# Two of four weight sums by accumulating DMAs, six feed-forward blocks begun early, GpSimd left with transfers

## The chip, the cores and the metric

One core of a Trainium2 chip runs the whole program. Its engines work side by side and wait for one another at semaphores: TensorE (PE, with its weight loads, PEld), VectorE (DVE), ScalarE (ACT), GpSimd (POOL) and SyncE (SP, which only issues transfers). SP's transfers and POOL's transfers are two queues; each is issued in order. The metric is the device time in microseconds (us), a median over runs.

## The reference, cut to what matters

```python
h = rms_norm(x, g_pre_mix) * (1.0 + scale_m) + shift_m          # x: 512 tokens x 2048
o = concatenate([mla_mixer(...), gla_mixer(...)]) @ w_out       # attention and a chunked recurrence
x = x + gate_m * rms_norm(o, g_post_mix)
h = rms_norm(x, g_pre_ffn) * (1.0 + scale_f) + shift_f          # "the second norm"
f = (silu(h @ w_ffn_gate) * (h @ w_ffn_up)) @ w_ffn_down        # 2048 -> 5632 -> 2048
x = x + gate_f * rms_norm(f, g_post_ffn)
```

The six vectors shift, scale and gate come from `silu(c) @ w_ada + b_ada`, 96 rows of 128 outputs. All is float32.

## The kernel before, in words

Every large product is made of float32r matmuls: each operand is split into a rounded part and a rest, and `mm3` (L212 to L216) issues three matmuls for one. A weight tile is split by `wparts` (L902 to L906): ACT casts 128x1024 floats into the rounded part, DVE subtracts (L905) to get the rest. The parts lie in a ring of eight `wh` tiles of 1024 columns. A weight block is loaded by `raw_of` (L908 to L911), 1 MB on SP's queue, into a ring of four `wr` tiles. All other tiles of 512 columns come out of one pool of 73 (`t2`).

The feed-forward products are done by a seven-product scheme (Strassen-Winograd) on 2x2 blocks. The products of the up stage are called q1, q2, q5, r7, r6, q4, r3. q1 and q2 need the first half of the tokens and the weights as they are (b11, b21). For the others sums of the weights are made in place in the `wr` tiles, in this order of use: q5 needs b11+b12, r7 needs b12+b22, r6 needs b11+b12+b22, q4 needs all of them plus b21, and r3 needs b22 as it is. These are the "four sums of weights". Two are on DVE (`vadd`, L924) and two on POOL (`padd`, L921).

The program, in the order in which it is written (a scheduler then interleaves the engines' lists):

- Up to about 765 us: conditioning rows (`ada`, one load and one DVE reduction each, 64 of them handed out by `next(more)` beside the later projections), projections, attention, recurrence, and the first half of the output product.
- `out_group` (L875): the output product, for two tokens' tiles at a time, with the running squares and a product with the gate row on POOL (L887). `second_norm` (L793) follows for each token tile: it scales on DVE (L811), transposes on PE (L814), and its rows go through ACT (L820). `first_forms` and `more_forms` make seven token forms with their two parts, 56 tiles of the pool.
- The early loop (L928): for the first `PRO` blocks of 22, q1 and q2 alone, which need the first two token tiles only, with steps of the second norm and of the forms (`advance`) written in between. Its weights are loaded once more when the block is finished.
- The up loop (L969): per block two halves s of up to seven products, 2.87 us of PE each; after every two blocks `pair_forms` writes seven forms in two parts (14 tiles `gd`, 256 KB each) to memory through POOL's queue.
- The down loop (L1029): five groups of four blocks, each in two halves p of seven products. `back` (L1023, its transfer L1025) reads the 28 `gd` tiles of a group through SP's queue; the weights' sums are like those above, in 128x2048 tiles, two on DVE and two on POOL.
- The tail (L1074 on): the last two blocks by plain products, with the weights' rests made on POOL (L1084), the gate product on POOL (L1102), and the output.

Of the kernel before, what the change touches and what calls it, by code (L numbers as in the profile page):

```python
# [11 lines left out]
F32 = mybir.dt.float32  # L12
# [17 lines left out]
NBLK = DFF // 256  # L30
PRO = 2
ATT_SCALE = 192.0 ** -0.5
# [45 lines left out]
def block_kernel(ctx, tc, x, c, pos, w_ada, cols, w_g1, w_kqvr, w_uq, w_uk, w_uv, wg17,  # L78
# [373 lines left out]
    def fill_qk():  # L452
        for half in range(2):
            pss = [bank("A") for _ in range(4)]
            for kq in (2, 3):
                w = load_split(w_kqvr[half, kq], 4, 512)
                for k, b in ORDER[kq == 3]:
                    mm3(pss[b], cut(w[k], b * P, P), hT[4 * kq + k], kq + k == 2, kq + k == 6)
                if kq == 3:
                    add_up(pss, qk[4 * half:4 * half + 4])  # L460
                    qk[4 * half:4 * half + 4] = spill(qk[4 * half:4 * half + 4], "qk")
                yield

    def fill_vr():
        for ci in range(4):
            pss = [bank("A") for _ in range(4)]
            k0 = 2 if ci < 2 else 0
            for kq in range(k0, 4):
                w = load_split(w_kqvr[2 + ci, kq], 4, 512)
                for _ in range(4):  # L470
                    next(more)
# [22 lines left out]
    def fill_out():  # L494
# [3 lines left out]
        for i, (n, q) in enumerate(todo):  # L498
            w = ahead
            if i < 7:  # L500
                ahead = load_split(w_out[todo[i + 1]], 4, 512)
            for _ in range(2):
                next(more)
# [289 lines left out]
    def second_norm(t):  # L793
# [15 lines left out]
        for n in range(4):  # L809
            y = t2()  # L810
            V.tensor_scalar(y, og[t][n], v2, None, op0=ALU.mult)  # L811
            ps = bank("B")
# [62 lines left out]
    def out_group(n, toks, steps=0):  # L875
# [7 lines left out]
        for t in toks:  # L883
            o = og[t][n] = fetch(og[t][n])
            V.tensor_tensor(out=o, in0=pss[t], in1=o, op=ALU.add)
            A.activation(pss[t], o, AF.Square, accum_out=osum[:, 4 * t + n:4 * t + n + 1])
            nc.gpsimd.tensor_tensor(out=o, in0=o, in1=ggm[n], op=ALU.mult)  # L887

# [31 lines left out]

    def padd(out, a, b):  # L921
        nc.gpsimd.tensor_tensor(out=out, in0=a, in1=b, op=ALU.add)  # L922

# [4 lines left out]
    for j in range(PRO):  # L928
        raws = [raw_of(w_fg[j, s]) for s in range(2)]
        q1, sg = t2(), t2()  # L930
        for f, o in (("a11", 0), ("a12", 1024)):
            ps = bank("A")
            for s in range(2):
                up_product(ps, wparts(raws[s][:, o:o + 1024]), f, s, s == 0, s == 1)
                advance(2 if j == 0 else 3)
            if f == "a11":
                A.copy(out=q1, in_=ps)
# [31 lines left out]
    for j in range(NBLK):  # L969
        pss = {}  # L970
        for s in range(2):
            gr, ur = raw_of(w_fg[j, s]), raw_of(w_fu[j, s])
            b11, b21, b12, b22 = gr[:, :1024], gr[:, 1024:], ur[:, :1024], ur[:, 1024:]

            def product(name, f, src, tag):
# [14 lines left out]
            else:  # L990
                q1, sg = early[j]
            vadd(b11, b11, b12)
            padd(b12, b12, b22)
            product("q5", "s1", b11, "A")
# [3 lines left out]
            if s == 1:  # L998
# [4 lines left out]
                vadd(c22, pss["q5"], w_)  # L1003
            padd(b11, b11, b21)
            product("q4", "a22", b11, "B")
# [17 lines left out]
    def back(d):  # L1023
        t = t2(F32R)
        dma(out=t.bitcast(F32), in_=d)  # L1025
        return t

    acc = [[{} for _ in range(2)] for _ in range(2)]
    for c_ in range(NBLK // 4):  # L1029
        fs = {}  # L1030
        for p in range(2):
# [19 lines left out]
            product("q2", "a12", b21)  # L1051
            padd(b11, b11, b12)
            padd(b12, b12, b22)
            product("r3", "s4", b22)
# [22 lines left out]
    for n in range(4):  # L1077
        raw = raw_of(w_fl[n])
        row = []
        for k in range(4):  # L1080
            hi, lo = t2(F32R), t2(F32R)
            r = raw[:, k * 512:(k + 1) * 512]
            A.copy(out=hi, in_=r)
            nc.gpsimd.tensor_tensor(out=lo, in0=r, in1=hi, op=ALU.subtract)  # L1084
            row.append((hi, lo))
        wl.append(row)
    fsum = cp.tile([P, 4 * NT + 1], F32, name="fsum")
    for t in range(NT):
# [5 lines left out]
        for j, (n, o, w) in enumerate(parts_):  # L1094
# [6 lines left out]
            A.activation(sq, f, AF.Square, accum_out=fsum[:, 4 * t + j:4 * t + j + 1])  # L1101
            nc.gpsimd.tensor_tensor(out=f, in0=f, in1=ggf[n][:, o:o + w], op=ALU.mult)  # L1102
        v = small(1, "v1")
# [62 lines left out]
```

## Time and profile before

| | us |
|---|---|
| median of 3 runs | 2258.38 (2248.99 to 2261.52) |
| the profiled execution, its own time | 2255.43 |
| its span, first to last instruction | 2253.7 |

| engine | busy us | share |
|---|---|---|
| PE | 2109.3 | 94% |
| PE weight loads | 1851.7 | 82% |
| DVE | 1764.0 | 78% |
| ACT | 907.7 | 40% |
| POOL | 540.4 | 24% |

The span leaves 1.7 us of the profiled time outside. A busy PE is not PE at full rate, since matmuls overlap and the granted clock varies; so a view of stretches also counts the matmuls in each, and a stretch in which they are densest serves as the measure of what PE could have done.

### The profile page before, as it was taken

Reading aid. Unit: us, or ns where it says so; the run is one execution under the profiler, and the core shown is the slowest. Engines: PE = TensorE matmul, PEld = TensorE weight load, DVE = VectorE, ACT = ScalarE, POOL = GpSimd, SP = SyncE. Lnnn points to the kernel's source line nnn. Section 1 sums busy time; section 2 is a strip of 40 time slices with the busy share of each in tenths; the row PEclk is TensorE's granted clock in tenths of the full one; section 3 lists DMA queues with packets and bytes.
Section 4 is the critical chain, followed back from the end, with each engine's and each line's share of the span. In section 5 each row is a group of like instructions: output and inputs, shape, how many; then the busy total and the mean of one; then the engine's idle time right before and its main releaser. Section 6 shows DMA issues by size and latency. Waiting matters only on the chain. (4 is left out here: it accounts for less than half of the span.)

```text
span 2253.7 us, 32197 instructions
## 1 busy us (share of the span) xinstructions
PE 2109.3 (94%) x12714; PEld 1851.7 (82%) x12714; DVE 1764.0 (78%) x2095; ACT 907.7 (40%) x1265; POOL 540.4 (24%) x436
## 2 busy tenths in 40 slices
PE   7999999996999967999999999999999799999977
PEld 5888777773888867999999999999999687777866
DVE  6885787886475778888888888887887669888984
ACT  5433222324233664444434434434444353333332
POOL 0000000000212332323333333333332232131136
PEclk9999999996999979999999999999999999999989
DMA  8882586885575742434434424433433647564334
GB/s 333 317 306 100 210 306 246 316 311 199 187 247 202 260 178 75 178 133 158 160 122 149 173 113 146 178 113 141 178 128 125 244 178 273 213 217 148 128 131 150
DMA packets 91578, 432.18 MB, mean 192 GB/s; under 512 B 12168, under 2 KB 12280, under 8 KB 54817
## 3 DMA queue, kind: packets, MB, share of 16 engines
q1 hardware_dynamic: 69840, 360.09, 44.0%
q0 software_dynamic: 21584, 70.02, 8.1%
q8 instruction: 100, 1.64, 0.3%
q14 instruction: 52, 0.43, 0.1%
q10 hardware_dynamic: 2, 0.01, 0.0%
HBM read 370.80 MB, written 59.26 MB: 191 GB/s over the span
## 5 line engine op out<-in xcount | busy, mean ns | idle before, releaser
L905 DVE TENSOR_TENSOR wh<-wr,wh 128x1024 fp32r<-128x1024 f32 x448 | 677.8, 1524 | 214.7 <-ACT wh L904 210.3
L904 ACT CAST wh<-wr 128x1024 fp32r<-128x1024 f32 x448 | 464.6, 1050 | 649.0 <-PE ps L215 247.1
L214 PE MATMUL ps<-t,wh 128*128 128x256 f32 x2464 | 705.1, 286 | 18.8 <-ACT wh L904 9.0
L216 PE MATMUL ps<-t,wh 128*128 128x256 f32 x2464 | 704.9, 286 | 12.1 <-DVE wh L905 11.9
L215 PE MATMUL ps<-t,wh 128*128 128x256 f32 x2464 | 703.6, 286 | 4.4 <-DVE t L832 4.4
L214 PEld LDWEIGHTS ps<-t,wh 128*128 128x128 f32 x2464 | 479.0, 194 | 22.5 <-ACT wh L904 11.4
L216 PEld LDWEIGHTS ps<-t,wh 128*128 128x128 f32 x2464 | 478.7, 194 | 15.5 <-DVE wh L905 15.2
L215 PEld LDWEIGHTS ps<-t,wh 128*128 128x128 f32 x2464 | 479.0, 194 | 5.8 <-DVE t L832 5.7
L922 POOL TENSOR_TENSOR wr<-wr 128x1024 f32<-128x1024 f32 x88 | 223.5, 2540 | 500.5 <-DVE wh L905 232.1
L228 DVE CUSTOM_DVE_ANT_0 wr<-wr,cB 128x2048 f32<-128x2048 f32 x96 | 219.2, 2285 | 41.1 <-DMA wr<-w_ada 41.0
L215 PE MATMUL ps<-wh,t 128*128 128x512 f32 x560 | 222.9, 398 | 22.1 <-DVE wh L905 22.1
L214 PE MATMUL ps<-wh,t 128*128 128x512 f32 x560 | 221.4, 396 | 11.4 <-DMA t<-gd 11.3
L216 PE MATMUL ps<-wh,t 128*128 128x512 f32 x560 | 219.9, 395 | 0.5 <-DMA t<-gd 0.5
L202 ACT CAST hi<-wr 128x1024 fp32r<-128x1024 f32 (+3 forms) x122 | 122.7, 1010 | 223.1 <-PE ps L215 134.1
L203 DVE TENSOR_TENSOR lo<-wr,hi 128x1024 fp32r<-128x1024 f32 (+3 forms) x122 | 145.1, 1193 | 67.0 <-ACT hi L202 66.5
L215 PE MATMUL ps<-t,hi 128*128 128x512 f32 x432 | 173.0, 400 | 3.1 <-DVE t L302 3.0
L922 POOL TENSOR_TENSOR wr<-wr,wr 128x2048 f32<-128x2048 f32 x20 | 102.6, 5129 | 303.1 <-DVE wh L905 198.7
L216 PE MATMUL ps<-t,lo 128*128 128x512 f32 x432 | 170.4, 395 | 0.0
L214 PE MATMUL ps<-t,hi 128*128 128x512 f32 x432 | 168.7, 398 | 1.3 <-ACT t L300 1.3
L214 PE MATMUL ps<-hi,t 128*128 128x512 f32 x400 | 161.4, 404 | 1.0 <-DVE t L209 0.9
L925 DVE TENSOR_TENSOR wr<-wr,wr 128x1024 f32<-128x1024 f32 (+1 forms) x108 | 153.3, 1420 | 5.5 <-DMA wr<-w_fu 3.2
L215 PE MATMUL ps<-lo,t 128*128 128x512 f32 x400 | 156.6, 392 | 0.3 <-DVE lo L203 0.3
(230 smaller groups left out, 2656.6 us busy)
## 6 DMA issues: line engine op xcount, KB each, us to landing
wr<-w_ada SPq DMA_DIRECT2D x96, 1024.0 KB, 5.8
wr<-w_fg SPq DMA_DIRECT2D x48, 1024.0 KB, 5.0
wr<-w_fu SPq DMA_DIRECT2D x44, 1024.0 KB, 7.2
wr<-w_fd SPq DMA_DIRECT2D x40, 1024.0 KB, 4.9
gd<-t POOLq DMA_DIRECT2D x148, 256.0 KB, 2.6
t<-gd SPq DMA_DIRECT2D x148, 256.0 KB, 5.3
wr<-w_kqvr SPq DMA_DIRECT2D x24, 1024.0 KB, 4.9
wr<-w_out SPq DMA_DIRECT2D x22, 1024.0 KB, 5.5
```

The source lines that it names most:

```text
L202: A.copy(out=hi[:, :n], in_=r)
L203: V.tensor_tensor(out=lo[:, :n], in0=r, in1=hi[:, :n], op=ALU.subtract)
L214: T.matmul(ps, lhsT=a, rhs=c_, start=start, stop=False)
L215: T.matmul(ps, lhsT=a, rhs=d_, start=False, stop=False)
L216: T.matmul(ps, lhsT=b, rhs=c_, start=False, stop=stop)
L228: V.tensor_tensor_reduce(out=raw, in0=raw, in1=cB, scale=1.0, scalar=0.0, op0=ALU.mult, op1=ALU.add, accum_out=adac[:, j:j + 1])
L904: A.copy(out=hi, in_=src)
L905: V.tensor_tensor(out=lo, in0=src, in1=hi, op=ALU.subtract)
L922: nc.gpsimd.tensor_tensor(out=out, in0=a, in1=b, op=ALU.add)
L925: V.tensor_tensor(out=out, in0=a, in1=b, op=ALU.add)
```

## The change

Accumulating DMAs (`plus`: a transfer on POOL's queue that adds what it reads from memory into the tile) make two of the four sums: b12+b22 and b11+b12, the addend being read from the weights in memory once more. They are issued on POOL's queue. The other two are DVE's. POOL has no arithmetic left: the gate products and the rests of the tail go to DVE, and the scaling by the second norm's factor goes from DVE to ACT. `back` is issued on POOL's queue instead of SP's. `PRO` is 6 instead of 2, with two steps of the norm at each place of the early loop. 16 of the 64 `ada` steps are handed out earlier, beside four sweeps that had none.

```diff
-PRO = 2
+PRO = 6
@@ fill_qk
                 w = load_split(w_kqvr[half, kq], 4, 512)
+                for _ in range(4):
+                    next(more)
@@ fill_vr
-                for _ in range(4):
+                for _ in range(3):
                     next(more)
@@ fill_out
-            for _ in range(2):
+            for _ in range(1 + q):
                 next(more)
@@ second_norm
-            V.tensor_scalar(y, og[t][n], v2, None, op0=ALU.mult)
+            A.activation(y, og[t][n], AF.Copy, scale=v2)
@@ out_group
-            nc.gpsimd.tensor_tensor(out=o, in0=o, in1=ggm[n], op=ALU.mult)
+            V.tensor_tensor(out=o, in0=o, in1=ggm[n], op=ALU.mult)
-    def padd(out, a, b):
-        nc.gpsimd.tensor_tensor(out=out, in0=a, in1=b, op=ALU.add)
+    def plus(out, src):
+        dma2(out=out, in_=src, accum_op=ALU.add)
@@ early loop
-                advance(2 if j == 0 else 3)
+                advance(2)
@@ up loop
             b11, b21, b12, b22 = gr[:, :1024], gr[:, 1024:], ur[:, :1024], ur[:, 1024:]
+            plus(b12, w_fu[j, s, :, 1024:])
@@
-            vadd(b11, b11, b12)
-            padd(b12, b12, b22)
+            plus(b11, w_fu[j, s, :, :1024])
             product("q5", "s1", b11, "A")
             product("r7", "s3", b12, "A")
             vadd(b11, b11, b22)
             product("r6", "s2", b11, "B")
@@
-            padd(b11, b11, b21)
+            vadd(b11, b11, b21)
             product("q4", "a22", b11, "B")
@@ back
-        dma(out=t.bitcast(F32), in_=d)
+        dma2(out=t.bitcast(F32), in_=d)
@@ down loop
-            padd(b11, b11, b12)
-            padd(b12, b12, b22)
+            plus(b11, w_fd[c_, 0, 2 * p + 1])
+            plus(b12, w_fd[c_, 1, 2 * p + 1])
             product("r3", "s4", b22)
@@ tail
-            nc.gpsimd.tensor_tensor(out=lo, in0=r, in1=hi, op=ALU.subtract)
+            minus(lo, r, hi)
-            nc.gpsimd.tensor_tensor(out=f, in0=f, in1=ggf[n][:, o:o + w], op=ALU.mult)
+            V.tensor_tensor(out=f, in0=f, in1=ggf[n][:, o:o + w], op=ALU.mult)
```

## Rows read from the trace of the kernel before

**Rows 1.** Stretches: length, PE (matmuls), PEld, DVE, ACT, POOL busy, clock, DMA, GB/s.

```profile
800.00:950.00 150.00, 119.77 (x875) 114.25 (x874) 124.51 (x158) 73.42 (x126) 44.42 (x35) 0.89 0.42 153
950.00:1000.00 50.00, 50.00 (x418) 50.00 (x417) 37.96 (x34) 21.05 (x24) 12.88 (x5) 1.00 0.28 106
950.00:1730.00 780.00, 765.69 (x6290) 761.75 (x6289) 647.14 (x607) 333.42 (x383) 256.67 (x201) 0.99 0.39 143
1750.00:1800.00 50.00, 37.16 (x174) 29.82 (x172) 35.12 (x28) 20.80 (x28) 14.08 (x10) 0.93 0.62 234
1800.00:2140.00 340.00, 323.61 (x1396) 264.79 (x1397) 285.81 (x237) 130.66 (x134) 80.68 (x16) 0.98 0.54 195
2120.00:2140.00 20.00, 20.00 (x90) 16.57 (x89) 19.76 (x24) 8.06 (x8) 0.00 (x0) 1.00 0.61 211
2140.00:2190.00 50.00, 40.01 (x168) 31.81 (x166) 46.97 (x49) 19.02 (x27) 12.92 (x4) 0.94 0.34 126
2190.00:2254.00 64.00, 49.05 (x203) 36.99 (x203) 27.61 (x57) 13.68 (x39) 42.05 (x37) 0.90 0.41 148
```

**Rows 2.** The hole of the second norm, same columns as rows 1.

```profile
820.00:845.00 25.00, 10.31 (x55) 8.62 (x55) 17.42 (x27) 19.74 (x49) 7.83 (x6) 0.61 0.49 191
```

**Rows 3.** SP's issues around it: start, us, queue, line, tile from source.

```profile
781.16 10.36 SPq L799 DMA_DIRECT2D wr<-x  x2
799.21 14.84 SPq L910 DMA_DIRECT2D wr<-w_fg  x3
```

**Rows 4.** PE's waits from 960 to 1720: us in total, times, longest.

```profile
PE ps L216 <- DVE wh L905: 9.1, 9, 1.0
PE ps L214 <- ACT wh L904: 5.2, 9, 0.6
```

**Rows 5.** PE's waits from 1720 on, same columns.

```profile
PE ps L215 <- DVE wh L905: 22.1, 12, 3.8
PE ps L215 <- POOL t L1084: 11.4, 12, 8.3
PE ps L214 <- DMA t<-gd: 11.3, 2, 6.5
```

**Rows 6.** POOL and DVE in order of time, in an up block (start, us).

```profile
1000.23 2.40 POOL L922 TENSOR_TENSOR wr<-wr 128x1024 f32<-128x1024 f32 x1 [6.79 <-issue]
...
1000.62 3.10 DVE L905 TENSOR_TENSOR wh<-wr,wh 128x1024 fp32r<-128x1024 f32 x1
...
1005.56 1.22 DVE L905 TENSOR_TENSOR wh<-wr,wh 128x1024 fp32r<-128x1024 f32 x1
```

**Rows 7.** POOL and DVE near the end of the down stage (start, us).

```profile
2143.86 12.11 POOL L922 TENSOR_TENSOR wr<-wr,wr 128x2048 f32<-128x2048 f32 x2 [36.94 <-DVE wh L905]
...
2147.11 9.94 DVE L905 TENSOR_TENSOR wh<-wr,wh 128x1024 fp32r<-128x1024 f32 x2
```

**Rows 8.** Groups by line and form: count, busy us, mean ns, idle before.

```profile
L922 POOL TENSOR_TENSOR wr<-wr 128x1024 f32<-128x1024 f32 x88 | 223.5, 2540 | 500.5 <-DVE wh L905 232.1 <-DVE wr L925 175.2 <-issue 93.0
L922 POOL TENSOR_TENSOR wr<-wr,wr 128x2048 f32<-128x2048 f32 x20 | 102.6, 5129 | 303.1 <-DVE wh L905 198.7 <-DMA wr<-w_fd 72.1 <-DMA t<-gd 31.6
L228 DVE CUSTOM_DVE_ANT_0 wr<-wr,cB 128x2048 f32<-128x2048 f32 x96 | 219.2, 2285 | 41.1 <-DMA wr<-w_ada 41.0
```

**Rows 9.** Transfers: SP's queue (packets, MB, share); issues with KB and us to landing.

```profile
q1 hardware_dynamic: 69840, 360.09, 44.0%
...
wr<-w_fu SPq DMA_DIRECT2D x44, 1024.0 KB, 7.2
...
gd<-t POOLq DMA_DIRECT2D x148, 256.0 KB, 2.6
```

**Rows 10.** SP's issues where the down stage begins, two of ten rows.

```profile
1748.36 10.64 SPq L1025 DMA_DIRECT2D t<-gd  x12
1777.95 0.33 SPq L910 DMA_DIRECT2D wr<-w_fd  x1
```

**Rows 11.** POOL in the tail, in order of time.

```profile
2191.80 19.85 POOL L1084 TENSOR_TENSOR t<-wr,t 128x512 fp32r<-128x512 f32 x16
```

## The prediction

> **What bounds the kernel now.** I read the stretches first. PE is busy nearly everywhere, so the question is how far each stretch is from PE's own best. In 950 to 1000 us there are 418 matmuls of 256 columns in 50 us without a gap, 0.1196 us each; in 2120 to 2140, in the down stage, 90 of 512 columns in 20 us, 0.222 us each [rows 1]. These two are the measure: a stretch's length less its count times the measure is what it loses, be it in gaps, in a lower granted clock or in loose pairs. All numbers are of the profiled execution (2255.4 us; span 2253.7, 1.7 outside), 3 us under the median of 2258.4.
>
> - 800 to 950, second norm and first up blocks: 875 matmuls at 0.1196 make 104.7 of 150 us: **45 lost**.
> - 950 to 1730, the up loop: 6290 make 752 of 780: **28 lost**.
> - 1750 to 1800, up to down: 51 of the 174 are still of the small kind: 6.1 + 123 x 0.222 = 33.4 of 50: **17 lost**.
> - 1800 to 2140, down: 1396 x 0.222 = 310 of 340: **30 lost**.
> - 2140 to 2190: 168 x 0.222 = 37.3 of 50: **13 lost**. From 2190 PE's work is some 43 us (203 matmuls, 24 of them small) and ends about 2245, so **12 lost**.
>
> That is 145 us, all in stretches that the change touches. Then the waits: who ends them.
>
> **The early blocks.** From 820 to 845 PE is busy 10.3 of 25 us, at a granted clock of 0.61 on average, so between its levels of 1.2 and 2.4 GHz [rows 2]: the two early blocks are used up and the forms of the last two token tiles aren't made. An early block is 96 small matmuls (2 products x 2 halves x 24), 11.5 us; four more are 46 us of work that waits for none of those forms, against 45 lost. They cost 8 more loads of 1 MB, beside other work. What limits them is buffers: of four wr tiles two hold x from its issue at 781 to 791 until the norm is done, and the weights of the early blocks come in late, three issues from 799 to 814 [rows 3]. So not all of the hole fills: **28 gained**, bounds 8 (only what two wr tiles bring in time) and 42. DVE's y (16 scalings) going to ACT and the gate products coming from POOL (16) cancel on DVE; ACT has room there, 73.4 of 150 us busy [rows 1].
>
> **The sums in the up loop.** A POOL sum of 1024 columns takes 2.54 us, 88 times [rows 8], and DVE's subtraction issued beside one takes 3.10 us instead of 1.22 [rows 6]. Four sums a block cost DVE about 4 x 1.9 = 7.5 us of the block's 40.2 (336 x 0.1196). PE waits in this loop once for each pair of blocks, where pair_forms add DVE work: 9 times for the rest (9.1 us) and 9 times for the cast (5.2) [rows 4]; the other half of the 28 lost is slow restart after these. DVE's own count of sums stays (b21 comes, b12 goes), so all 7.5 us a block are relief and the pair's stall, 1.6 us, should go. **18 gained**, bound 25.
>
> What takes its place is an adding DMA's time. No row shows one. By length: the nearest rows are a store of 256 KB, 2.6 us to landing, and a load of 1 MB, 7.2 us [rows 9]; for 512 KB I take 6 us, nearer the load, since it reads memory and shares the queue. b11's add stands between the parts of q1 and of q5. At PE's pace that is two products, 5.7 us, and the ring of eight wh tiles lets parts be made up to four products, 11.5 us, ahead. Up to some 13 us it costs PE nothing; beyond it each half of a block loses the excess. Behind the waiting add on POOL's queue stand the spills of pair_forms, and their tiles come from a pool of 73 of which 56 are forms and now 12 are early results: about three are free at the first pair, where eleven were. There ACT and DVE can wait for a landed spill.
>
> By engine time: SP's queue moved 360 MB in 44.0% of 2253.7 us [rows 9], so 1 MiB takes all 16 engines 2.9 us. A half block loads 2 tiles (5.8), spills 3.5 of 14 quarter-MB tiles (2.6 with rounding up) and adds 1 MiB in two parts: 2.9 if an add costs as a copy, 5.8 if its second read costs like another copy. With the latter, 14.2 us of a half's 20.1. But blocks 0 to 5 have only five products a half, 14.35 us: there the transfers nearly fill the time, over 172 us, where before it was two blocks. I charge **10** for this and the first pairs; bounds 0 and 25.
>
> Here the Trainium skill speaks against the change: "Collectives: The Full Stack", section "The bandwidth ceiling", says that an add in the DMA engines needs two reads per chunk on one ring and measured 62.28 against 32.35 GB/s, copy against add. By that an add costs about 1.93 copies, a half block 5.6 instead of 2.9 us for its adds, and the short blocks are at their limit; no row of before shows an add, so nothing here bears it out yet.
>
> **Up to down.** SP issues w_fd and gd tiles in one order: after the 12 gd issues that begin at 1748.4 the next comes at 1777.95, and it is the w_fd that waited for a wr tile, 19 us with gd tiles behind it [rows 10]. PE then waits 11.3 us for gd, twice [rows 5]. With `back` on POOL's queue that order is gone; but now gd reads stand behind the last spills and the first adds. **8 gained** of 17, bounds 0 and 15.
>
> **Down.** A POOL sum of 2048 columns takes 5.1 us [rows 8] and holds DVE as long: two such beside two subtractions, 9.94 us for 2.4 [rows 7]. DVE is busy 286 of 340 us [rows 1], PE waits for rests 22.1 us from 1720 on [rows 5]. Both sums leave; DVE's own count stays. b11's add has three products, 16 us, before q5. But the transfers: a half group (168 matmuls, 37.3 us) has 4 loads (11.6), 14 gd reads (10.2) and 2 MiB of adds, 5.8 to 11.6, so 27.6 to 33.4 us, where the row shows a share of 0.54. **12 gained** of 30, bounds -10 and 25.
>
> **End of down and tail.** The 12.1 us of POOL sums at 2144 go [rows 7]: 6 gained. POOL's 16 rests of the last weights take 19.85 us in one run from 2191.8 [rows 11], after gate rows that wait for DVE; PE waits 11.4 us for them [rows 5]. On DVE one takes about 0.6 us (half of the 1.22 of rows 6), ahead of PE's pace of 12 matmuls, 2.6 us, for four. 8 gained. **14** in all, bounds 5 and 20. The last gate products don't move the end.
>
> **The conditioning rows.** 16 of 64 reductions of 2.285 us [rows 8] move earlier, beside sweeps that had none; their number is the same. Costed at nothing, with 8 us either way, since the order of DVE changes there; what hides them is PE's backlog, and without it each would cost its 2.3 us.
>
> **The sum.** 28 + 18 + 8 + 12 + 14 - 10 = 70. 2255.4 - 70 = 2185 on the profile's basis, 2188 on the median's.
>
> **The rivals.**
>
> - *Half the gain.* The early blocks starve for wr and t2 tiles (8 instead of 28), and POOL's single queue gives back what it frees up (up to down 0, down 5, charge 15): 8 + 18 + 0 + 5 + 14 - 15 = 30, so 2228. For it: rows 3, and adds, spills and reads in one order. Against: POOL loses 540 us of work less its issues. This is also the case in which the six blocks aren't begun in time.
> - *Slower: adds fill the DMA engines.* Say an add costs k copies. The down half is full from 5.8k + 21.8 = 37.3, k = 2.7; a short half from 8.4 + 2.9k = 14.35, k = 2.1; the long half only from k = 4. At k = 4 the short blocks lose 12 x 5.7 = 68 us and down 10 x 7.7 = 77; with the other gains left (28 + 18 + 8 + 14 = 68) that is 77 slower, 2335. It turns at about k = 3.2. For it: an add must read, read and write. Against: share 0.39 to 0.54 now [rows 1].
> - *All gaps close.* The upper bounds, 42 + 25 + 15 + 25 + 20 = 127: 2131. For it: every loss has the POOL sums or SP's order as its cause. Against: each new wait would have to be hidden.
>
> **How the numbers follow.** Forecast 0.60, half the gain 0.18, all gaps 0.10, adds too dear or too late 0.12. The forecast's own range by its bounds is 2150 to 2225. The range with the rivals: up to 2255, which takes in the half gain and leaves out most of the slow case, and down to 2140: 2140 to 2255. What a measurement of this kernel can tell from no change is about 0.5%, 11 us: faster means under 2247. Faster: 0.60 + 0.10 + 0.12 of the half gain = 0.82; same 0.07; slower 0.11.
>
> **What would show it.** Right: DVE's subtractions at 1.22 us throughout; no pair stall in the up loop and 418 matmuls per 50 us; no hole and full clock from 820 to 845; no wait for L1084. Wrong: PE or ACT waiting for a wr tile whose last writer is an adding DMA, a landing over 13 us, a DMA share near 1 in the short blocks or the down stage, or DVE waiting for a pool tile at the first pair. The forecast falls if an add costs over three copies, or if the early blocks' weights come no sooner than now.

## The result, and the profile after

| | before | after |
|---|---|---|
| median, us | 2259.72 (2248.99 to 2261.52) | 2369.65 (2362.69 to 2371.69) |
| ratio, 95% interval | | 1.0491 [1.0452, 1.0531] |
| span of the profiled execution, us | 2253.7 | 2369.9 |

The forecast was 2188 us, in 2140 to 2255. The change made the kernel 110 us slower. Where the time went can be read by taking, in both traces, the start of the n-th matmul in PE's order (both kernels have 12714). From the seventh block on this is the same matmul in both; at n = 4500 it is only the same amount of work, since four more blocks have been begun:

```
n        where                        before us   after us   difference   in this part
 4500    the up loop has just begun       971.3      956.4       -14.8        -14.8
10500    near the end of the up loop     1716.7     1820.6      +103.9       +118.7
11500    down loop, two fifths over      1933.6     2067.6      +134.0        +30.1
12500    near the end of the down loop   2182.3     2295.6      +113.3        -20.7
12713    last matmul                     2245.0     2360.7      +115.8         +2.5
```

So the loss lies in the up loop (119 us) and at the turn to the down loop with its first two fifths (30 us). The stretches show the same. The columns are those of rows 1: length, busy time and count of PE, PEld, DVE, ACT and POOL, granted clock, DMA share, GB/s.

```profile
1400.00:1450.00 50.00, 42.87 (x338) 41.85 (x337) 26.47 (x28) 15.83 (x17) 3.52 (x5) 0.97 0.57 159
...
2050.00:2100.00 50.00, 50.00 (x222) 41.42 (x221) 39.10 (x39) 19.64 (x19) 10.35 (x18) 1.00 0.83 271
```

In the up loop 338 matmuls fit where 418 did [rows 1]; DVE is busy about half of that time, ACT a third, the DMA engines 0.57. Nothing is full: this is the picture of a chain, not of a bound engine. In the down loop, PE runs at its measure with the adds in it, 222 in 50 us.

The page of after shows what the engines do on average (count, busy us, mean ns, idle before and its releaser), then the up loop's adds by KB and median us to landing, those into b11 and b12 together:

```profile
L907 DVE TENSOR_TENSOR wh<-wr,wh 128x1024 fp32r<-128x1024 f32 x448 | 539.1, 1221 | 479.7 <-ACT wh L906 455.7
...
L906 ACT CAST wh<-wr 128x1024 fp32r<-128x1024 f32 x448 | 459.9, 1049 | 746.0 <-DMA wr<-w_fu 323.7
...
wr<-w_fu POOLq DMA_DIRECT2D x88, 512.0 KB, 5.6
```

DVE's subtraction takes 1221 ns in the mean of all 448, as forecast (3.10 us beside a POOL sum in rows 6). But ACT's cast, the first step of every weight tile, now waits 323.7 us for `wr<-w_fu`. The waits of the up loop, 1100 to 1850 us (us in total, times, longest), say which transfer that is and how it reaches PE:

```profile
POOL wr L924 <- DVE wh L907: 331.8, 30, 17.0
ACT wh L906 <- DMA wr<-w_fu: 294.1, 30, 11.6
...
PE ps L216 <- DVE wh L907: 43.3, 50, 1.5
PE ps L214 <- ACT wh L906: 41.5, 24, 4.3
```

L924 is the adding DMA. POOL holds b11's add until DVE has made q1's parts out of b11, and ACT stops until the add has landed, 30 times, once in each half of a block. One turn of this, on SP's queue, then POOL's, then ACT's and DVE's (start, us, tile, count, idle before):

```profile
1420.34 0.33 SPq L912 DMA_DIRECT2D wr<-w_fg  x1
1421.47 0.33 SPq L912 DMA_DIRECT2D wr<-w_fu  x1
```

```profile
1422.87 0.86 POOL L924 DMA_DIRECT2D wr<-w_fu  x1 [15.15 <-DVE wh L907]
1430.08 0.85 POOL L924 DMA_DIRECT2D wr<-w_fu  x1 [6.34 <-DMA wr<-w_fu]
1446.47 0.86 POOL L924 DMA_DIRECT2D wr<-w_fu  x1 [15.54 <-DVE wh L907]
```

```profile
1432.12 1.99 ACT L906 CAST wh<-wr 128x1024 fp32r<-128x1024 f32 x2 [9.56 <-DMA wr<-w_fu]
...
1436.27 1.05 ACT L906 CAST wh<-wr 128x1024 fp32r<-128x1024 f32 x1 [0.58 <-DVE wr L927]
1441.60 2.95 ACT L906 CAST wh<-wr 128x1024 fp32r<-128x1024 f32 x3 [4.28 <-DVE wr L927]
1444.90 1.05 ACT L906 CAST wh<-wr 128x1024 fp32r<-128x1024 f32 x1 [0.35 <-PE ps L215]
```

SP issues the next two loads of 1 MB at 1420 to 1421, when the tiles of the half before come free. The add into b11 goes out at 1422.87 and has landed when ACT goes on at 1432.12, 9.25 us later. Only then can q5's parts be made, and after them, in the fixed order of ACT and DVE, those of r7, the sum for r6, its parts, the sum for q4, its parts, r3's and the next q1's: the next add goes out at 1446.47, 14.35 us after the landing. The add that is issued at 1430.08 is b12's: it waited for its own load, has little ahead of it, and lands in 5.4 us. A turn of landing and leg is 23.6 us here; the half's 168 matmuls need 20.1.

Between the loops POOL's queue shows the second loss (`t<-gd`, L1027, are the loads of stored forms, now POOL's):

```profile
1865.52 0.85 POOL L924 DMA_DIRECT2D wr<-w_fd  x1 [26.37 <-DVE t L834]
...
1879.74 2.87 POOL L1027 DMA_DIRECT2D t<-gd  x5 [4.36 <-DMA wr<-w_fd]
...
1894.88 1.80 POOL L1027 DMA_DIRECT2D t<-gd  x3 [0.45 <-issue]
1922.54 0.90 POOL L924 DMA_DIRECT2D wr<-w_fd  x1 [25.85 <-DVE wh L907]
1923.10 2.52 POOL L1027 DMA_DIRECT2D t<-gd  x4
...
1975.03 1.77 POOL L924 DMA_DIRECT2D wr<-w_fd  x2 [48.48 <-DVE wh L907]
1976.17 3.88 POOL L1027 DMA_DIRECT2D t<-gd  x6
```

At the turn the queue's head waits 26 us for a part that `pair_forms` makes (L834); the first loads go out behind it, two adds and the stores between them at 1879.74, and PE, which waits for them, goes on at 1885.60 after 22 us. Later loads stand behind adds that wait 26 and 48 us for DVE's parts. DVE's parts wait for PE, and PE waits for the loads, 11 us each time. PE's only large wait from 1850 us to the end:

```profile
PE ps L214 <- DMA t<-gd: 61.6, 4, 22.0
```

Three of the four are here (44.2 us); the fourth, 17.4 us, is in the tail, where the last loads stand behind the gate rows in the same queue.

### The profile page after: what moved, and what is told of

Read it like the earlier page. It is cut to its first block, busy times and chain, and to the rows that moved or that the text cites. A ratio compares the mean times of both kernels' runs of the same rounds, so it can differ in the third digit from the quotient of the medians.

```text
span 2369.9 us, 32048 instructions
## 1 busy us (share of the span) xinstructions
PE 2134.3 (90%) x12714; PEld 1873.1 (79%) x12714; DVE 1610.1 (68%) x2128; ACT 912.9 (39%) x1277; POOL 322.9 (14%) x535
## 5 line engine op out<-in xcount | busy, mean ns | idle before, releaser
L907 DVE TENSOR_TENSOR wh<-wr,wh 128x1024 fp32r<-128x1024 f32 x448 | 539.1, 1221 | 479.7 <-ACT wh L906 455.7
L214 PE MATMUL ps<-t,wh 128*128 128x256 f32 x2464 | 717.4, 291 | 64.4 <-ACT wh L906 46.7
L216 PE MATMUL ps<-t,wh 128*128 128x256 f32 x2464 | 718.8, 292 | 50.5 <-DVE wh L907 50.0
L906 ACT CAST wh<-wr 128x1024 fp32r<-128x1024 f32 x448 | 459.9, 1049 | 746.0 <-DMA wr<-w_fu 323.7
L215 PE MATMUL ps<-t,wh 128*128 128x256 f32 x2464 | 711.2, 289 | 0.0
L214 PEld LDWEIGHTS ps<-t,wh 128*128 128x128 f32 x2464 | 488.2, 198 | 73.6 <-ACT wh L906 54.5
L216 PEld LDWEIGHTS ps<-t,wh 128*128 128x128 f32 x2464 | 487.4, 198 | 63.6 <-DVE wh L907 63.6
L215 PEld LDWEIGHTS ps<-t,wh 128*128 128x128 f32 x2464 | 488.2, 198 | 0.0
L214 PE MATMUL ps<-wh,t 128*128 128x512 f32 x560 | 221.0, 395 | 44.2 <-DMA t<-gd 44.2
L924 POOL DMA_DIRECT2D wr<-w_fu x88 | 76.2, 866 | 755.2 <-DVE wh L907 371.8
L927 DVE TENSOR_TENSOR t<-ps,t 128x512 f32<-128x512 f32 x222 | 150.1, 685 | 21.1 <-PE ps L216 20.4
L214 PEld LDWEIGHTS ps<-wh,t 128*128 128x128 f32 x560 | 106.9, 191 | 67.5 <-issue 45.1
```

The lines of the kernel that those rows point to most:

```text
L214: T.matmul(ps, lhsT=a, rhs=c_, start=start, stop=False)
L215: T.matmul(ps, lhsT=a, rhs=d_, start=False, stop=False)
L216: T.matmul(ps, lhsT=b, rhs=c_, start=False, stop=stop)
L906: A.copy(out=hi, in_=src)
L907: V.tensor_tensor(out=lo, in0=src, in1=hi, op=ALU.subtract)
L924: dma2(out=out, in_=src, accum_op=ALU.add)
```

## The experiments

Each run is compared with runs of the kernel before on the same chip; its medians there lie between 2256.6 and 2259.9, so runs of different chips can be set side by side to within some 4 us. e1 and e4 rest on two executions each, 10 and 6 us apart, the others on four to ten. By n is again meant the n-th matmul in PE's order.

| run | what it is | median, us | ratio to before, 95% |
|---|---|---|---|
| | the change | 2369.65 | 1.0491 [1.0452, 1.0531] |
| e1 | up loop: all sums on DVE | 2232.94 | 0.9874 [0.9807, 0.9940] |
| e2 | e1, the adds issued on dead tiles | 2250.17 | 0.9947 [0.9924, 0.9971] |
| e3 | r3 put behind b11's add | 2244.53 | 0.9931 [0.9904, 0.9958] |
| e4 | stored forms loaded by SP | 2332.67 | 1.0315 [1.0263, 1.0366] |
| e7 | e1 and e4 together | 2188.46 | 0.9696 [0.9668, 0.9723] |
| e8 | e3 and e4 together | 2206.10 | 0.9774 [0.9746, 0.9802] |
| e9 | e7, two early blocks | 2178.29 | 0.9656 [0.9629, 0.9684] |
| e10 | e7, the down loop's sums on DVE too | 2182.98 | 0.9671 [0.9644, 0.9698] |
| e11 | before, its POOL sums on DVE | 2195.57 | 0.9709 [0.9679, 0.9739] |
| e12 | e9 and e10 together | 2170.84 | 0.9603 [0.9574, 0.9631] |
| e13 | e4, b11's add alone in the up loop | 2335.26 | 1.0332 [1.0300, 1.0365] |
| e14 | e13 with half of the add's bytes | 2289.56 | 1.0119 [1.0078, 1.0160] |
| e15 | e4, raw loads from POOL by the add | 2263.93 | 1.0026 [1.0007, 1.0046] |
| e16 | e4, b11's add made a plain load | 2265.54 | 1.0026 [1.0003, 1.0048] |
| e17 | e7, raw loads from POOL | 2190.61 | 0.9698 [0.9670, 0.9726] |
| e18 | e4, raw loads behind the add's landing | 2216.36 | 0.9816 [0.9784, 0.9847] |

### A chain through b11's add, or full DMA engines?

Theory: the chain shown above. Rivals: the bytes of the adds, VectorE, or the order in POOL's queue.

**e1**, the sums of the up loop on DVE:

```diff
-            plus(b12, w_fu[j, s, :, 1024:])
...
-            plus(b11, w_fu[j, s, :, :1024])
+            vadd(b11, b11, b12)
+            vadd(b12, b12, b22)
```

> After, with all four sums of the up loop on VectorE (vadd) and no adding DMA there; the down loop keeps its adds. Theory, the chain: in the changed kernel a half of an up block takes 24.6 us (168 matmuls at 0.1463) because the parts of q5 wait for b11's add, some 9 us from issue to landing, and the add waits for the parts of q1, which stand behind q4's and r3's in ACT's and DVE's order. Without it a half falls to 20.1 to 20.8 us; 32 long halves times 3.8 to 4.5 give 120 to 145 us: 2225 to 2250. DVE gets two sums more, 2.4 us a half, about 17 of 20.1. Rival, bytes: the adds' traffic fills the DMA engines; gone too, the same time, so this run alone doesn't tell them apart. Rival, DVE becomes the bound: the half stays over 22 us and the time over 2290.

2232.94 us: the adds of the up loop cost 137 us, and DVE takes all four sums.

**e2**, the same adds on tiles that nobody reads any more:

```diff
             product("r7", "s3", b12, "A")
+            plus(b12, w_fu[j, s, :, 1024:])
...
             product("q4", "a22", b11, "B")
+            plus(b11, w_fu[j, s, :, :1024])
```

> As e1 (all four sums on VectorE), with the same two adding DMAs per half kept, but issued when their tile is dead (b12 after r7's parts, b11 after q4's parts), so that the traffic and POOL's queue are as in the changed kernel and no product reads what they write; only the tile's next load waits. The output is not touched. Theory, the chain: as fast as e1, within 20 us. Rival, bytes: the DMA engines are what is short, 24 us a half stay: 2350 to 2375. Rival, POOL's order (spills of pair_forms behind waiting adds): stays in part, 2290 to 2340.

2250.17, 17 us above e1. The same transfers, nobody waiting for the sums, cost an eighth of the loss: the bytes are not its cause. From n = 6500 to 10500 e2 takes 480.0 us, as e1 does. Its 17 us go earlier, in the blocks of five products: 268.6 us from n = 4500 to 6500, against 248.1. There the next load of a tile waits for the dead add, and the DMA share from 950 to 1100 us is some 0.8, against 0.5 in e1; which of the two costs the time isn't told apart.

**e3**, all adds kept, one product moved:

```diff
             plus(b11, w_fu[j, s, :, :1024])
+            product("r3", "s4", b22, "B")
             product("q5", "s1", b11, "A")
...
-            product("r3", "s4", b22, "B")
```

> The changed kernel with one product moved: r3 (b22, needs no sum) stands between q2 and q5 instead of last, as in the down loop, so that one more product lies between b11's add and its use and one fewer between q4's parts and the next q1's. Everything else, bytes too, is the same. Theory, the chain: about 2.9 us more cover per half; of the 4.5 us that a half lies over PE's 20.1, 2.5 to 4 go: 80 to 125 us, 2245 to 2290. Rival, bytes: no change, 2360 to 2375. Rival, POOL's order: no change.

2244.53, half a us under the theory's range: 125 of the 137 us come back by order alone. r3 needs no sum; its parts are made while the add is under way, and the leg behind the landing is one product shorter. That is only a part of the gain. The add also lands sooner, in a median of 6.6 us from 1250 to 1700 us against 9.3 in the change: with r3 moved, SP's load of w_fg goes out 7 to 9 us ahead of the add and has landed when the add is issued, and only that of w_fu is still ahead of it. The chain is shown; why its landing is so long comes below.

### The one queue

**e4**, in `back`:

```diff
-        dma2(out=t.bitcast(F32), in_=d)
+        dma(out=t.bitcast(F32), in_=d)
```

> The changed kernel with the reads of gd (back) on SP's queue again. Theory, one queue: POOL's queue holds the reads of the first group's tiles behind adds that wait for a later product's parts (POOL idle 48 us before an add at 1975), and at the tail behind the gate rows; PE waits 61.6 us for gd in all. On SP these go, 40 to 55 us: 2315 to 2330. Rival: the old order on SP (reads behind a load that waits for a wr tile) gives as much back, 11 us of the wait before and more with tiles held longer by adds: 2345 to 2370.

2332.67, 37 us less, where the theory had 40 to 55: it is the queue, with a little less than booked. PE's waits for `t<-gd` fall from 61.6 to 16.9 us.

**e7** is e1 with that line, **e8** is e3 with it.

> The change without its two adding DMAs in the up loop (all four sums there on VectorE), and with the loads of the stored parts (t<-gd) issued by SyncE again instead of GpSimd. Theory, two independent costs: the chain through b11's add and the one queue of GpSimd. With sums on VectorE alone the kernel stood at 2233 us with 57.2 us of TensorE waits for t<-gd in its trace; SyncE gave back 37 us to the unaltered change. So 2185 to 2205 us, and under 20 us of waits for t<-gd. Rival, that the waits between the up and the down loop are the transfers themselves (stored parts, weights and parts at once) and not the queue they are issued from: 2220 to 2235 us, the waits staying above 40 us.

> The change with both adding DMAs of the up loop kept, but the product r3 (which needs no sum) put between q2 and q5, and the loads of the stored parts issued by SyncE. Theory, chain: with r3 in the add's shadow the up loop is free of it, as at 2244.5 us with 60.6 us of waits for t<-gd; the queue's 37 to 45 us come off that: 2198 to 2212 us. If adding DMAs cost the up loop something besides the chain (engine time, the queue of GpSimd), it stays 15 us or more above the kernel with all up sums on VectorE and the same loads by SyncE (run in this call); if only the chain cost, the two lie within 10 us of each other.

2188.46 and 2206.10, both in the ranges of the theory. The two costs add: 137 and 37 make 174, and the two repairs together gave 181. The 18 us between e8 and e7 lie in the long blocks, 497.3 against 480.0 us from n = 6500 to 10500, where e2's dead adds cost nothing: they are what r3 leaves of the chain. ACT still waits 104 us for adds from 1250 to 1700 us in e8, in 16 of some 21 halves, and 3608 matmuls fit there, against 3752 in e7. PE's waits for the weights' parts from 750 to 2160 us, 2.3 and 2.7 us in e7, are in e8:

```profile
PE ps L216 <- DVE wh L907: 11.4, 16, 0.9
...
PE ps L214 <- ACT wh L906: 8.4, 6, 2.5
```

PE's waits for `t<-gd` from 750 to 2160 us in e7, under the 20 us of the theory:

```profile
PE ps L214 <- DMA t<-gd: 9.8, 3, 4.8
...
PE ps L216 <- DMA t<-gd: 6.0, 3, 3.5
```

### The parts that were booked as gains

**e9**, e7 with the early loop of before:

```diff
-PRO = 6
+PRO = 2
...
-                advance(2)
+                advance(2 if j == 0 else 3)
```

> The kernel with all up sums on VectorE and loads by SyncE (run in this call), with two blocks begun beside the second norm instead of six (and the norm's steps spread over them as before). The prediction booked 28 us gained beside the norm for the four further blocks and 10 us of charge for short blocks. Theory, the blocks are worth what was booked: 15 to 30 us slower than with six. Rival, the work beside the norm only comes earlier and the up loop is bound as before per block: within 5 us of the same kernel with six.

2178.29: not slower but 10 us faster (2177.30 to 2180.00, against 2182.88 to 2191.43 with six), which is neither case of the expectation. The stretches of e7 (six blocks), then of e9 (two):

```profile
800.00:850.00 50.00, 32.49 (x240) 30.56 (x238) 31.04 (x59) 40.08 (x85) 4.34 (x8) 0.86 0.52 185
850.00:900.00 50.00, 41.26 (x315) 41.09 (x316) 38.96 (x48) 25.26 (x37) 0.00 (x0) 0.87 0.31 117
...
950.00:1000.00 50.00, 47.68 (x380) 47.05 (x380) 46.65 (x54) 20.41 (x24) 7.54 (x14) 0.97 0.50 183
1000.00:1050.00 50.00, 48.68 (x401) 48.01 (x400) 47.23 (x54) 20.54 (x24) 7.55 (x14) 1.00 0.61 229
```

```profile
800.00:850.00 50.00, 31.06 (x204) 28.37 (x202) 39.50 (x70) 39.29 (x82) 4.34 (x8) 0.80 0.48 168
850.00:900.00 50.00, 46.69 (x367) 45.77 (x367) 45.73 (x52) 22.70 (x29) 0.00 (x0) 0.97 0.31 110
...
950.00:1000.00 50.00, 50.00 (x419) 50.00 (x418) 41.35 (x45) 22.71 (x27) 5.62 (x11) 1.00 0.35 137
1000.00:1050.00 50.00, 50.00 (x419) 50.00 (x418) 42.06 (x42) 22.08 (x24) 1.93 (x4) 1.00 0.41 148
```

With six blocks PE does 36 matmuls more in the first 50 us and 52 fewer in the next: the hole is not filled but moved. The later stretches then show the price: blocks of five products a half keep DVE at 93 to 94% of the time for 380 and 401 matmuls, against 83 to 84% for 419. PE's waits of e7 from 800 to 900 us name who holds it:

```profile
PE ps L214 <- ACT t L939: 9.1, 2, 7.0
PE ps L214 <- DVE t L927: 8.6, 1, 8.6
PE ps L816 <- ACT t L813: 7.5, 4, 3.6
```

L939 is the early blocks' own copy of q1 on ACT and L927 the DVE sum that adds it to q2: both stand in the same two engines' order as the norm's scaling (L813), which makes 15.8 of PE's 22.1 us of waits in e9. The new work waits for the engines for which the old work waits. That more blocks in another order of these steps could not do better isn't shown.

**e10**, e7 with `vadd(b11, b11, b12)` and `vadd(b12, b12, b22)` in the place of the down loop's two adds:

> The kernel with all up sums on VectorE and loads by SyncE (run in this call), with the two adding DMAs of the down loop replaced by VectorE sums too, so that no sum is made by a DMA and none by GpSimd. In the trace with the adds a stretch of 50 us of the down loop holds 222 matmuls without a gap and VectorE is busy for 38.6 us of it; a pass over one p is 12.6 us, so four passes bring 8 more sums of 1.2 to 1.4 us, 10 to 11 us, and VectorE comes to 96 to 100%. Theory, the adds are what holds the down loop at TensorE's pace: 5 to 20 us slower, with waits of TensorE for VectorE's parts in that loop. Rival, VectorE still fits: within 4 us.

2182.98, 5 us under e7, with ranges that overlap: not slower. The theory, that only the adds let the down loop run at PE's pace, falls. In e10, from 1850 us:

```profile
1850.00:1900.00 50.00, 50.00 (x222) 41.42 (x221) 44.93 (x43) 18.89 (x18) 0.00 (x0) 1.00 0.84 306
```

All sums are DVE's, DVE has 5 us of 50 to spare, PE has no gap. The gain in the down loop came from POOL's leaving, not from the DMAs.

**e11**, the kernel before with one word changed:

```diff
     def padd(out, a, b):
-        nc.gpsimd.tensor_tensor(out=out, in0=a, in1=b, op=ALU.add)
+        V.tensor_tensor(out=out, in0=a, in1=b, op=ALU.add)
```

> The kernel before with nothing but the engine of its sums changed: what GpSimd added (padd) is added by VectorE, so all four sums of a half or a pass are VectorE's, none by a DMA, two blocks begun early, everything else as before. Theory: the gain behind the start of the pair blocks comes from taking GpSimd's adds from beside VectorE (2540 ns against 1222 ns for VectorE's own add), whoever makes them. From that point on the kernel without adding DMAs and the kernel with them only in the down loop won 58 and 59 us on the kernel before, by the time of the same matmul; so some 59 us under the kernel before: 2190 to 2207 us. Rival, that VectorE fills up without the other's help and that the gain needs a place off both engines: 2235 us or more.

2195.57, as the theory had it: 64 us of gain with no DMA that adds, no other queue and no further early block. DVE makes 108 more sums and is better off, since its 448 subtractions are short again:

```profile
L905 DVE TENSOR_TENSOR wh<-wr,wh 128x1024 fp32r<-128x1024 f32 x448 | 541.9, 1222 | 166.0 <-ACT wh L904 163.1
```

**e12** is the change without its adds, without POOL's `back` and without the four further early blocks.

> The change with all sums in both loops on VectorE, stored parts loaded by SyncE, and two blocks begun early: of the change only what comes ahead of the pair blocks is left, and GpSimd free of arithmetic. Two against six blocks was worth 10 us, VectorE's sums in the down loop 5 us more: 2170 to 2178 us. Rival, the two overlap, since both end in the same waits for stored parts: 2178 to 2184 us.

2170.84 us, 0.9603 [0.9574, 0.9631]: the fastest kernel of the study. Beyond e11 it has the earlier conditioning rows, the norm's scaling on ACT, and gate products and last rests on DVE; they are worth 13 us at n = 4500 and 11 us in the tail. The 13 us are there at n = 2500 already (596.5 against 611.0 us). From n = 500 to 2500 the change alters only when the conditioning rows are handed out; there the two kernels with the old order, before and e11, take 480.1 and 485.1 us, and all sixteen with the new one 464.2 to 477.9, about 470 in the median. So the earlier rows are what gains here. From n = 2500 to 4500 e12 takes 356.5 us and e11 355.2: scaling and gate products beside the norm are worth nothing by that.

### Why does b11's add take so long to land?

**e13**, b11's add alone (b12's sum by `vadd`), loads of stored forms by SP.

> The change with SyncE loading the stored parts, and of the up loop's two adding DMAs only the one into b11, which q1's parts hold back; b12's sum on VectorE. With both adds this stood at 2332.67 us, with none at 2188.46. Theory, chain: b11's add alone makes the loss, through its wait for q1's parts and its landing beside the next loads: 2295 to 2335 us. Rival, the two adds share the loss because both take the DMA engines: some 2260 us.

2335.26, the upper end of the theory's range: the one add makes the whole loss. **e14** lets the DMA add half of the columns:

```diff
-            plus(b11, w_fu[j, s, :, :1024])
+            plus(b11[:, :512], w_fu[j, s, :, :512])
+            vadd(b11[:, 512:], b11[:, 512:], b12[:, 512:])
```

> As the kernel with the one add into b11, but the DMA adds only half of b11's columns, 256 KB; VectorE adds the other half and b12. The wait for q1's parts and the place in the order are the same; only the landing is shorter. Theory, chain: 14.35 us from landing to the next issue and, from 8.2 to 9.4 us for 512 KB beside two loads, an estimated 4 to 6 us for half of it, 18.4 to 20.4 us against a half's 20.1 us of matmuls: the loss mostly goes, 2190 to 2225 us. Rival, the landing is latency that bytes hardly change (a fixed cost of an accumulating DMA, or of standing behind the loads): within 25 us of the kernel with the whole add.

2289.56: between the two cases. Half the bytes took back 46 of 147 us; its landing fell only from a median of 9.3 to 7.6 us. My estimate of 4 to 6 us for the landing was wrong: most of it doesn't go with the bytes. **e16** makes b11's add a plain load, so that the sum is left out, and is otherwise e4:

```diff
-            plus(b11, w_fu[j, s, :, :1024])
+            dma2(out=b11, in_=w_fu[j, s, :, :1024])
```

> The change with SyncE loading the stored parts, and b11's add turned into a plain load of the same 512 KB into the same place at the same point of the order: the sum of b11 with the second block is left out. Theory, any transfer of that size in the middle of the chain, behind the two raw loads, costs most of the loss; it takes the engines about what half the add takes (which gave 2289.56): 2270 to 2310 us. Rival, the loss is the accumulation itself (its second read and the write back): within 25 us of 2188, the kernel with no add in this loop.

2265.54, 5 us under the theory's range and 77 over e7, far from the rival's. So a transfer in this place costs about half of the loss without any accumulation; the accumulation adds 67 us (e4). **e15** was to put the raw loads behind the add:

```diff
             plus(b11, w_fu[j, s, :, :1024])
+            if (j, s) != (NBLK - 1, 1):
+                ahead2 = both(j + s, 1 - s)     # gr, ur of the next half, by dma2
```

> The change with SyncE loading the stored parts and both adds of the up loop kept; the two raw loads of 1 MB of the following half are issued from GpSimd right behind b11's add, instead of from SyncE 1 to 2.5 us ahead of it. Nothing else moves. Theory, the landing is long (8.1 to 9.4 us) because the add stands behind those loads; b12's adds, issued when the loads have landed, take 5.3 to 5.6 us. With that landing the chain is 14.35 + 5.5 = 19.9 us against a half's 20.1: the loss goes, 2190 to 2235 us. Rival, the landing is the add's own in this place, whatever stands ahead: 2305 to 2340 us, as with the loads ahead (2332.67).

> Control for the loads issued from GpSimd: the same place of the raw loads, all four sums of the up loop on VectorE, no adding DMA in that loop. Theory: within 10 us of 2188.46, the same kernel with the loads from SyncE; what the kernel with adds behind differs from this one is then the adds alone. Rival, GpSimd's one queue, with the stores of gated pairs between the loads, delays the loads: 2205 us or more.

The control e17 is at 2190.61, 2 us from e7: the loads may be POOL's. e15 came to 2263.93, between the two cases, and its trace says why; POOL in order of time:

```profile
1203.63 0.54 POOL L974 DMA_DIRECT2D wr<-w_fg  x1 [6.49 <-DVE wh L907]
1205.66 0.90 POOL L924 DMA_DIRECT2D wr<-w_fu  x1 [1.49 <-DVE wh L907]
1206.22 0.90 POOL L974 DMA_DIRECT2D wr<-w_fu  x1
```

The scheduler issued at least one load ahead of the add. By the trace, of b11's adds from 1090 to 1760 us the seven with both loads ahead landed in 8.8 to 9.8 us, the eight with one load and six stores of `pair_forms` ahead in 7.7 to 9.0, and the fifteen with one load alone in 5.4 to 7.4. So the run changed less than it was meant to. **e18** forces the order: the loads go into tiles that wait for the add.

```diff
             raw = wp.tile([P, 2048], F32, tag="wr", name=nm("wr"))
+            if after is not None:               # after: b11 of this half, behind its add
+                V.tensor_copy(out=raw[:, 0:8], in_=after[:, 0:8])
             dma(out=raw, in_=src)
```

> The change with SyncE loading the stored parts and both adds kept; each of the next half's two raw tiles first gets eight columns copied by VectorE from b11 behind its add (and overwritten by the load), so that the 1 MB loads can only be issued when the add has landed. Theory: a half takes 14.35 us and the landing. So far that gives 23.5 us at a landing of 9.2 (found 143 us lost in 44 halves beside the kernel without adds, 23.4 a half), 21.9 at 7.5 with half the bytes (found 22.2) and 21.7 at 7.3 with the plain load (found 21.9). With nothing ahead b11's add lands in 5.1 to 5.6 us as b12's does: 19.8 us, under the 20.1 of its matmuls, and the up loop is free: 2188 to 2215 us. Rival, the landing is the add's own in this place: 2300 to 2340 us; or the loads now come too late for q1's parts (5 to 9 us from landing against 12 to q1's parts): over 2225 us with ACT waiting for w_fg.

2216.36, 116 us under e4 and 1 us over the theory's range; both rivals fall. The adds' landings from 1250 to 1700 us (min, median, max), in e13 and then in e18:

```profile
L924 POOL DMA_DIRECT2D wr<-w_fu x18: 851/878/908, 1270.0 to 1697.5; - x18
...
DMA to landing us min/median/max: 7.5/9.3/10.7
```

```profile
L924 POOL DMA_DIRECT2D wr<-w_fu x44: 848/867/942, 1250.6 to 1697.7; - x44
...
DMA to landing us min/median/max: 5.1/5.4/8.3
```

The stretch from 1250 to 1700 us gives the length of a half: 450 us times 168 by the count of matmuls. In e13, e14, e16, e18 and e7, in this order:

```profile
1250.00:1700.00 450.00, 394.30 (x3058) 382.83 (x3057) 293.77 (x316) 160.92 (x188) 53.75 (x88) 0.95 0.47 146
```

```profile
1250.00:1700.00 450.00, 407.12 (x3225) 398.18 (x3224) 327.27 (x356) 168.44 (x196) 55.53 (x90) 0.97 0.43 143
```

```profile
1250.00:1700.00 450.00, 417.66 (x3343) 411.09 (x3342) 297.35 (x324) 176.89 (x204) 66.48 (x110) 0.98 0.57 182
```

```profile
1250.00:1700.00 450.00, 439.03 (x3595) 434.13 (x3594) 326.48 (x391) 189.45 (x221) 80.68 (x121) 1.00 0.68 195
```

```profile
1250.00:1700.00 450.00, 450.00 (x3752) 450.00 (x3751) 389.09 (x408) 203.56 (x229) 41.05 (x76) 1.00 0.41 153
```

| run | landing of b11's transfer, median us | a half, us | half less landing, us |
|---|---|---|---|
| e13, whole add | 9.3 | 24.7 | 15.4 |
| e14, half of it | 7.6 | 23.4 | 15.8 |
| e16, plain load | 7.3 | 22.6 | 15.3 |
| e18, no load ahead | 5.4 (both adds) | 21.0 | 15.6 |
| e7, no add | | 20.15 | |

A half is the landing plus 15.3 to 15.8 us. One leg of it stood above with 14.35; the mean is longer, since in every fourth half the work of `pair_forms` stands between. Taken from one landing to the next issue, the legs are much the same in kernels with very different landings: 12.7 to 14.8 us and 19.9 in every fourth half in e16, 12.7 to 15.4 and 19.8 in e18. The room for a landing is therefore 20.1 - 15.5 = 4.6 us, and no add of 512 KB landed in that.

## Why the prediction was wrong

**The step that failed** is the one on the sums in the up loop: "Up to some 13 us it costs PE nothing". It took the ring of eight `wh` tiles as room for four products, 11.5 us, which the add could use up. But what comes ahead of q5 while the add is under way, q1 and q2, is made by then (in the turn above ACT idles from 1422.56 on, 0.3 us before the issue), and the leg goes on behind the landing: the parts of a half are made one after another, with the sums that build on b11 between them, and end in the next q1's parts, for which the next add waits. By the table the limit was 4.6 us, not 13. The right question was not how much work lies in the add's shadow but how long the loop is that leads from one add to the next: landing, q5, r7, r6, q4, r3, q1, issue. Its length without the landing, 15.5 us, could have been estimated beforehand: six casts of 1.05, six subtractions and two sums of 1.22 us are 16.1, if all stood one behind another.

**The landing.** "For 512 KB I take 6 us" is about right for an add with no load ahead (a median of 5.4 us) and 3 us short in the place where it matters. The add is released by the same progress that frees the tiles, so SP's two loads go out 1.4 to 4.4 us ahead of it in every half from 1100 to 1750 us. The prediction had the loads in its sum of engine time, and not in the landing.

**The charge** for all this was 10 us; the adds of the up loop cost 137 (e1). The engine-time argument behind it held: an add is about two copies (e4 and e16 differ in nothing but the accumulation of 23.07 MB; POOL's queue takes 23.4% of 2327.8 us in the one, 21.2% of 2271.8 in the other, 63 us apart; a plain copy of these bytes at the rate of SP's queue in e4, 368.48 MB in 44.1%, is 64 us: 1.98 copies; SP's own bytes, the same in both, took 18 us less in e16, so this is good to about 0.3). The rows of e4, then of e16:

```profile
q1 hardware_dynamic: 70992, 368.48, 44.1%
q0 software_dynamic: 37136, 137.13, 23.4%
```

```profile
q1 hardware_dynamic: 70992, 368.48, 44.4%
q0 software_dynamic: 37136, 137.13, 21.2%
```

By the rates that the Trainium skill's "Collectives: The Full Stack", section "The bandwidth ceiling", gives for a collective's copy and add, it would be 1.93, an estimate: the trace agrees. So the slower rival had the sign but not the mechanism; it turned at 3.2 copies. The sum for a short half, 14.2 of 14.35 us, came out as well. From 1000 to 1050 us the change has:

```profile
1000.00:1050.00 50.00, 49.17 (x410) 48.97 (x409) 37.70 (x42) 18.98 (x22) 12.79 (x20) 1.00 0.95 286
```

The engines are at 0.95, one of the signs of error that the prediction named, and yet PE does 410 matmuls there, where e7 without these adds does 401. The loss lies where the share is 0.57. Of the other signs, ACT waiting for a `wr` tile whose last writer is an adding DMA is what came; the threshold beside it, a landing over 13 us, was the wrong one.

**Up to down, 8 gained**, was a loss of 30 (with the first two fifths of the down loop), and in the tail PE waited 17 more for the same queue. The rival "half the gain" had the mechanism, one queue of POOL, but priced it at giving back what it frees. A queue whose head waits for what PE's progress releases, with loads behind it for which PE waits, costs whole waits, here of 11 to 22 us. Moving `back` to SP gave 37 (e4).

**The early blocks, 28 gained**, gave nothing: two in the place of six were 10 us faster (e9). The hole was read as PE lacking work; the engines that prepare the work, ACT and DVE, were what it lacked. The short blocks did cost something, but not by the path that was charged: with no add in the up loop six blocks take 8 us more than two from n = 4500 to 6500 (e7, e9), at a DVE that is 93 to 94% busy.

**What held.** The relief of DVE: 18 in the up loop, bound 25, against 25 in e11 (from -5.1 at n = 4500 to -30.5 at 10500). Down loop and its end, 12 + 6: 20.7 in the change, 18.5 in e11 (n = 11500 to 12500). The rests of the tail, 8: 11 in e12 against e11. The conditioning rows, costed at nothing, gained some 10 to 15 us (see e12). With 25 + 18 + 11 and the early part of 13 the forecast of 70 was within reach, and e12's 89 is past it: but it takes leaving the adding DMAs out.

**Open.** e18 is still 28 us behind e7. By the table a half is 0.9 us over that of e7, and 32 halves of that length make 28; its legs are close to those of e16, and landings of 5.6 us in the mean with legs of 15.3 make up the 21.0, so this is still the chain. That no other order of the loads and products could take the rest away isn't shown. Why transfers ahead lengthen the landing, by sharing the engines or by a completion that waits for earlier writes, wasn't tried. The Trainium skill's "DMA: Bandwidth & Descriptors", section "Issuing engines are not separate DMA queues", says that transfers of all issuing engines run on the same 16 engines and interleave; the landings agree: 5.4 us with no load ahead, 9.3 with two loads on another queue.

## What to carry to other kernels

When an operation is handed to a DMA inside a loop, follow the loop from one issue to the next and add up everything on it, the landing among whatever the same event releases; compare that with the time of one turn, and don't count work in its shadow or engine shares. If that sum is too long, put independent work behind the issue (e3: one product moved, 125 us, a part of it by a shorter landing), or hold the other loads back (e18: 116 us). And before work is taken off two engines that slow each other, try giving all of it to the one that is hurt (e11: one word, 64 us).

## What the runs showed of the hardware that was not expected

- DVE, given 108 further sums, was busy for less time than before, 1741 against 1764 us (e11): its subtraction, 3.10 us beside a POOL sum [rows 6], took 1.22 us in the mean (1.52 before), and a DVE sum of 1024 columns takes 1.22 us against POOL's 2.54 [rows 8].
- The landing of an adding DMA goes only in part by its bytes: 256 KB 7.6 us, 512 KB 9.3 us, with the same two loads ahead; a plain load of 512 KB there 7.3. With no load ahead 512 KB were added in 5.4 us.
- An adding DMA's record on POOL is 0.87 us long, a plain one's 0.54, but the next issue began 0.56 us after an adding one, too (1922.54 and 1923.10 in the rows between the loops, 1205.66 and 1206.22 in e15).
